# A hybrid diffusion layer on one core: where the last gate's modulation is summed, and which engine does five small groups of the mixer

## The chip, the core and the metric

The kernel runs on one core of one Trainium2 chip. The core has a matrix engine (TensorE, PE in the profile, with its weight loads as PEld), a vector engine (VectorE, DVE), a scalar engine (ScalarE, ACT), a general-purpose engine (GpSimd, POOL) and a synchronisation engine (SyncE, SP) that here only starts DMA transfers. Each engine works through its own instruction queue in order and waits on semaphores for the others. The metric is the device time of one execution in microseconds, the median of several runs.

## The reference, cut to what matters

One layer: a half-step SwiGLU FFN, a token mixer (grouped-query attention and a bidirectional mLSTM side by side), a second half-step SwiGLU FFN, a final RMSNorm. Every sub-layer is normalised and then shifted, scaled and gated by rows of a modulation vector, which has nine rows of 2048.

```python
D_MODEL = 2048; SEQ = 256; CTX_LEN = 256; HEAD_DIM = 128; N_MOD = 9

def adaln(x, g, mod, i):
    return rms_norm(x, g) * (1 + mod[:, i + 1, None, :]) + mod[:, i, None, :]

def half_step_ffn(x, mod, i, g, w_up, w_down):
    h = adaln(x, g, mod, i)
    a, b = jnp.split(h @ w_up, 2, axis=-1)
    return x + 0.5 * mod[:, i + 2, None, :] * ((jax.nn.silu(a) * b) @ w_down)

def reference(...):
    mod_l = (silu_c @ w_mod[l] + b_mod[l]).reshape(B, N_MOD, D_MODEL)
    xl = half_step_ffn(xl, mod_l, 0, ...)
    ...
    xl = xl + mod_l[:, 5, None, :] * mixer_output(att_l, hm_l, ...)
    xl = half_step_ffn(xl, mod_l, 6, ...)
    return rms_norm(xl, g_final)
```

Row 8 of the modulation is the gate of the second FFN: it is first used when the second FFN's last sums are gated. Row 5 gates the mixer's output, rows 6 and 7 shift and scale the second FFN's input. In the mLSTM, keys carry a factor of 128 to the power -0.5, ISQ in the kernel.

## The kernel before, in words

All weights are fp32. A product is made of three matmuls in the fp32r format: the weight is split into a rounded part `hi` and a rest `lo`, and hi times hi, hi times lo and lo times hi are summed (`mm3`, lines 145 to 149). The split of one weight tile of 128 x 2048 (`split`, lines 117 to 136) is made in two halves, each one ACTIVATE by ScalarE (line 125) and one subtraction by VectorE (line 126), into rings of four halves for hi and four for lo. `load_split` (line 138) loads a tile by SyncE, splits it, and lets a side stream called `beside["load"]` go one step.

The mixer (lines 1259 to 1855) projects in this order, each weight tile feeding 24 or 48 matmuls: w_c, w_a, w_b (values and gates of the mLSTM, four groups of tokens), w_mk and w_mq (keys and queries of the mLSTM, eight heads each, with a short convolution), w_kv, w_q0, w_o0, w_o1, w_q1 (attention and output gates), and the output projection w_out, three quarters of it first (`out_proj` with weights 2, 0, 3 for each of four column blocks), the last quarter after attention. Between the matmuls, generators are stepped by hand: mLSTM states, `latents`, `attention`, `evacs`. `tc.keep_in_program_order` ties an instruction behind the previous one traced on its engine; what is not tied may be moved by a list scheduler, which goes by its own estimate of when each instruction is ready.

The modulation rows 2 to 8 are not made by matmuls. For each row i, each block of 128 outputs (kt, 16 of them) and each half h of the 2048 inputs, a tile of 128 x 1024 of w_mod is loaded (512 KB) and VectorE multiplies it with the broadcast condition vector and sums along the row, in one SCALAR_TENSOR_TENSOR (`mod_half`, line 205). Such an instruction is called a pass here. Rows 2 to 4 are done in the first FFN (`mod_items`), rows 5 to 7 in the mixer (class `Beside`, lines 271 to 337), row 8 in the second FFN (`mod_late`, lines 264 to 269, stepped by `load_split` there). When all 32 passes of a row are done, `mod_end` adds halves and bias, and for a gate row `mod_rows_out` turns it by a transpose on TensorE and writes it to DRAM.

`Beside` holds its tiles in six buffers: sr0, sr1, sr2 and three that lie in memory which later stages need. Each buffer has a limit, the number of the first pass that may not use it: N_EARLY for the three that lie in mqT and rt, N_MIXER for sr1 and sr2. At the end of the mk stage `mods.close(N_EARLY)` issues all passes below that number, before the output projection `mods.close(N_MIXER)` does, and then three further buffers in mkT and C1 are added (line 1787). The pass order is h first, then row, then kt; at the change of h the condition vector is loaded again. A pass and the load into its buffer are tied to program order. When pass n is issued is set by PACE, pairs (n, step) that are interpolated; a step is taken after each contraction block of a projection with tokens still (16 steps each), after four of them in mk and mq (4 per head), and after each weight tile of the output projection (12). Each h adds WAIT = 3 steps.

```python
                    if self.n not in self.slots or self.done < np.interp(self.n, *zip((0, 0), *self.pace)) + self.waits:
                        break
                    self.one()
```

The second FFN (lines 1858 to 2253) interleaves blocks computed directly (`up`, `down`) with blocks by a seven-product scheme (`quad`), whose token forms (`token_forms`, line 2010) are made by VectorE and ScalarE at its start. `before_final` (line 2227) ends the side stream of row 8 and loads the gate row.

The five groups of the mixer that the change touches: `state` scales the values with the input gates into vw (line 1429) and copies the state C1 out of PSUM (line 1434); the mq stage multiplies the convolved query by ISQ (line 1552); `attention` scales the probabilities p by their inverse sum sd (line 1699); `mlstm_cat` copies transposed heads cx out of PSUM (line 1750). All are VectorE's. In `latents` VectorE multiplies A with the query (line 1509) and E with the scores pS (line 1514).

Of the kernel before, what the change touches and what calls it, by code (L numbers as in the profile page):

```python
# [9 lines left out]
F32 = mybir.dt.float32  # L10
# [3 lines left out]
AF = mybir.ActivationFunctionType  # L14
ALU = mybir.AluOpType
# [4 lines left out]
P = 128  # L20
D = 2048
KT = D // P
T = 256
# [12 lines left out]
PACE = (4, 2), (12, 13), (19, 19), (26, 28), (33, 37), (37, 44), (42, 51), (48, 54), (52, 61), (55, 70), (58, 76), (59, 85), (63, 96)  # L36
PACE += (70, 102), (72, 109), (75, 118), (76, 130), (77, 144), (80, 152), (83, 163), (85, 166), (86, 174), (96, 181)

# [18 lines left out]
def tile_layer(ctx: ExitStack, tc: tile.TileContext, I: dict, out: bass.AP):  # L57
# [205 lines left out]

    def mod_late(sp, i0, i1, pace):

        cB = sp.tile([P, 1024], F32, name="cBl", bufs=1)
        cond = Conditions(lambda h: h, lambda h: conditions({LAT: cB}, h, h + 1, (LAT,)), lambda h: {LAT: cB})
        raws = lambda: sp.tile([P, 1024], F32, tag="sraw", name="sraw", bufs=2)
        return mod_items(half_items(i0, i1), nc.sync.dma_start, raws, 2, cond, None, pace)
# [131 lines left out]
    def drain(it):  # L401
        for _ in it:
            pass
# [855 lines left out]
    with ExitStack() as mx:  # L1259
# [31 lines left out]
        N_EARLY, N_MIXER = 50, 85  # L1291

        early2 = one([P, 2, 1024], "early2", tag="mqT")
        tiles = [(mm.tile([P, 1024], F32, name="sr0"), 96)] + [(mm2.tile([P, 1024], F32, name=f"sr{j}"), N_MIXER) for j in (1, 2)]
        tiles += [(x, N_EARLY) for x in (early2[:, 0, :], early2[:, 1, :], one([P, 1024], "early1", tag="rt"))]
        mods = Beside(mm, 5, 8, tiles, PACE)
# [122 lines left out]
        def state(h, kTc):  # L1419
# [7 lines left out]
            for t in range(2):  # L1427
                for d in range(2):
                    nc.vector.tensor_scalar(vw[:, t, d, :], v1[CTX][t][:, h, :], wg[:, t, d, h : h + 1], None, op0=ALU.mult)
# [4 lines left out]
            nc.vector.tensor_copy(C1[:, h, :, :], b[:, :260].rearrange("p (d c) -> p d c", d=2))  # L1434
# [39 lines left out]
        def latents():  # L1474
            held = {}
            for h in range(NH + 1):
                if h < NH:
# [31 lines left out]
                    nc.vector.tensor_tensor(A, A, mqT[:, h, :].unsqueeze(1).to_broadcast([P, 2, T]), op=ALU.mult)  # L1509
                    for d in range(2):  # L1510

                        for w, p0 in ((slice(0, 2), 0), (slice(2, 3), 3)) if d == 0 else ((slice(0, 1), 0), (slice(1, 3), 2)):
                            e_ = E[:, d, w, :]
                            nc.vector.tensor_tensor(e_, e_, pS.rearrange("p (q c) -> p q c", q=4)[:, p0 : p0 + w.stop - w.start, :], op=ALU.mult)
# [26 lines left out]
        for h in range(NH):  # L1541
# [8 lines left out]
            nc.scalar.activation(y, y, AF.Silu)  # L1550

            nc.vector.tensor_scalar(mqT[:, h, :], y, ISQ, None, op0=ALU.mult)
# [130 lines left out]
        def attention(kv):  # L1683
            items = [(t, g) for t in range(2) for g in range(4)]
            pr, pT, o = {}, {}, {}
            for i in range(len(items) + 2):
                if i < len(items):
# [11 lines left out]
                    nc.vector.tensor_scalar(p, p, sd, None, op0=ALU.mult)  # L1699
# [42 lines left out]
        def mlstm_cat(c):  # L1742

            for t in range(2):
# [5 lines left out]
                nc.vector.tensor_copy(cxs[c, t], tb)  # L1750
# [657 lines left out]
```

## Time and profile before

| | |
|---|---|
| median of three runs | 2613.49 us (2612.78 to 2615.28) |
| span of the profiled execution, first to last instruction | 2612.7 us |
| granted TensorE clock, mean over the span | 0.996 |
| HBM read, written | 659.87 MB, 17.89 MB |
| mean DMA rate over the span | 259 GB/s |
| mixer, projection a to the end of the output projection | 1395.7 to 1895.8 us |
| passes on VectorE in that stretch | 96, of 1.22 us each |

The profiled execution's time is shown by its span alone; the timed runs are 0.04 to 2.5 us above it. Times in the profile are counted from the first instruction of the span. A row of a group reads: line of the kernel, engine, operation, output<-inputs with their shapes, count; then busy us, mean ns of one, and the idle time of the engine just before such instructions with what ended it. A row of the timeline reads: start, duration (both us), engine, line, operation, names and shapes; in square brackets the engine's idle time before it and what ended it. Matmuls overlap their successors, so their durations exceed the distance between their starts.

### The profile page before, as it was taken

Reading aid. Unit: us, or ns where it says so; the run is one execution under the profiler, and the core shown is the slowest. Engines: PE = TensorE matmul, PEld = TensorE weight load, DVE = VectorE, ACT = ScalarE, POOL = GpSimd, SP = SyncE. Lnnn points to the kernel's source line nnn. Section 1 sums busy time; section 2 is a strip of 40 time slices with the busy share of each in tenths; the row PEclk is TensorE's granted clock in tenths of the full one; section 3 lists DMA queues with packets and bytes.
Section 4 is the critical chain, followed back from the end, with each engine's and each line's share of the span. In section 5 each row is a group of like instructions: output and inputs, shape, how many; then the busy total and the mean of one; then the engine's idle time right before and its main releaser. Section 6 shows DMA issues by size and latency. Waiting matters only on the chain.

```text
span 2612.7 us, 33775 instructions
## 1 busy us (share of the span) xinstructions
PE 2590.1 (99%) x12742; PEld 2158.4 (83%) x12742; DVE 2119.7 (81%) x2860; ACT 1364.8 (52%) x1734; POOL 205.2 (8%) x261
## 2 busy tenths in 40 slices
PE   8999999999999999999999999999999999999998
PEld 5788888888888888888889889888898888888887
DVE  7788888878888788888887879788888777777867
ACT  4454444454444465444454337555576655555554
POOL 0000000100000100010110000120000000000001
PEclk8999999999999999999999999999999999999999
DMA  9989999999999998889987856665679998989975
GB/s 389 353 215 266 280 273 274 257 273 284 265 277 277 271 246 237 231 200 232 231 247 262 300 193 236 220 214 208 236 254 302 309 293 278 286 285 283 270 231 174
DMA packets 127219, 679.97 MB, mean 260 GB/s; under 512 B 14152, under 2 KB 16712, under 8 KB 65232
## 3 DMA queue, kind: packets, MB, share of 16 engines
q1 hardware_dynamic: 99696, 500.59, 51.6%
q0 software_dynamic: 27360, 177.22, 34.7%
q8 instruction: 100, 1.64, 0.2%
q14 instruction: 63, 0.52, 0.1%
HBM read 659.87 MB, written 17.89 MB: 259 GB/s over the span
## 4 chain that ended last, share of the span: by engine, by line
PE 92%; DVE 3%; DMA 2%; issue 1%; ACT 1%; POOL 0%; ACTq 0%; POOLq 0%; SPq 0%; DVEq 0%
PE mm L147 24%; PE mm L149 24%; PE mm L148 24%; PE mm L85 2%; PE tr L147 2%; PE tr L149 2%; PE tr L148 2%; PE Y L149 1%; PE Y L147 1%; PE Y L148 1%; PE tr L85 1%; PE X L147 1%; PE X L149 1%; PE X L148 1%; DVE lo L126 1%
## 5 line engine op out<-in xcount | busy, mean ns | idle before, releaser
L125 ACT ACTIVATE hi<-raw 128x1024 fp32r<-128x1024 f32 (+3 forms) x536 | 556.4, 1042 | 594.7 <-PE mm L149 435.4
L126 DVE TENSOR_TENSOR lo<-raw,hi 128x1024 fp32r<-128x1024 f32 (+1 forms) x524 | 632.1, 1211 | 272.3 <-ACT hi L125 246.9
L125 ACT ACTIVATE hi<-chain 128x1024 fp32r<-128x1024 f32 x320 | 338.0, 1059 | 257.3 <-PE mm L149 133.9
L126 DVE TENSOR_TENSOR lo<-chain,hi 128x1024 fp32r<-128x1024 f32 x320 | 386.5, 1221 | 85.4 <-ACT hi L125 82.3
L147 PE MATMUL mm<-hi,hhi 128*128 128x512 f32 (+3 forms) x1024 | 393.8, 385 | 0.0
L148 PE MATMUL mm<-lo,hhi 128*128 128x512 f32 (+3 forms) x1024 | 386.8, 378 | 0.0
L149 PE MATMUL mm<-hi,hlo 128*128 128x512 f32 (+3 forms) x1024 | 386.8, 378 | 0.0
L205 DVE SCALAR_TENSOR_TENSOR junk<-sraw,cBh 128x1024 fp8e5<-128x1024 f32 x192 | 234.4, 1221 | 16.8 <-DMA sraw<-in_w_mt 14.4
L149 PEld LDWEIGHTS mm<-hi,hlo 128*128 128x128 f32 x1024 | 192.5, 188 | 33.9
L147 PEld LDWEIGHTS mm<-hi,hhi 128*128 128x128 f32 x1024 | 192.6, 188 | 31.0
L148 PEld LDWEIGHTS mm<-lo,hhi 128*128 128x128 f32 x1024 | 192.8, 188 | 30.6
L149 PE MATMUL mm<-hi,hid2l 128*128 128x512 f32 x352 | 137.4, 390 | 0.0
L147 PE MATMUL mm<-hi,hid2h 128*128 128x512 f32 x352 | 137.2, 390 | 0.0
L148 PE MATMUL mm<-lo,hid2h 128*128 128x512 f32 x352 | 137.1, 389 | 0.0
L148 PE MATMUL mm<-lo,h2hi 128*128 128x512 f32 x320 | 124.9, 390 | 0.6 <-DVE lo L126 0.6
L147 PE MATMUL mm<-hi,h2hi 128*128 128x512 f32 x320 | 124.8, 390 | 0.0
L149 PE MATMUL mm<-hi,h2lo 128*128 128x512 f32 x320 | 124.6, 389 | 0.0
L735 POOL DMA_DIRECT2D chain<-in_w_up1b x60 | 53.1, 886 | 726.4 <-DVE lo L126 699.5
L147 PE MATMUL mm<-hhi,hi 128*128 128x512 f32 (+1 forms) x288 | 101.1, 351 | 0.0
L149 PE MATMUL mm<-hhi,lo 128*128 128x512 f32 (+1 forms) x288 | 99.0, 344 | 0.0
L148 PE MATMUL mm<-hlo,hi 128*128 128x512 f32 (+1 forms) x288 | 98.8, 343 | 0.0
L205 DVE SCALAR_TENSOR_TENSOR sr<-sr,cBl 128x1024 f32<-128x1024 f32 x65 | 78.4, 1219 | 9.0 <-DMA sr<-in_w_mt 9.0
(517 smaller groups left out, 5466.9 us busy)
## 6 DMA issues: line engine op xcount, KB each, us to landing
raw<-in_w_dn SPq DMA_DIRECT2D x70, 1024.0 KB, 7.7
sraw<-in_w_mt SPq DMA_DIRECT2D x128, 512.0 KB, 7.7
chain<-in_w_up1b POOLq DMA_DIRECT2D x60, 1024.0 KB, 10.4
raw<-in_w_up2b SPq DMA_DIRECT2D x50, 1024.0 KB, 6.9
raw<-in_w_up1b SPq DMA_DIRECT2D x40, 1024.0 KB, 7.7
mraw<-in_w_m SPq DMA_DIRECT2D x32, 1024.0 KB, 7.8
sr<-in_w_mt SPq DMA_DIRECT2D x62, 512.0 KB, 5.4
chain<-in_w_dn POOLq DMA_DIRECT2D x30, 1024.0 KB, 9.4
```

The source lines that it names most:

```text
L85: ins = getattr(self.engine, name)(*a, **k)
L125: scalar[0].activation(hi, src, AF.Copy)
L126: vector[0].tensor_tensor(lo, src, hi.bitcast(F32), op=ALU.subtract)
L147: tensor[0].matmul(out_ap, sh, mh, start=first, stop=False, skip_group_check=skip)
L148: tensor[0].matmul(out_ap, sh, ml, start=False, stop=False, skip_group_check=skip)
L149: tensor[0].matmul(out_ap, sl, mh, start=False, stop=last, skip_group_check=skip)
L205: ins = nc.vector.scalar_tensor_tensor(junk() if junk else raw, raw, 1.0, cB[s], op0=ALU.mult, op1=ALU.mult, accum_out=mT[:, i, s, kt, h : ...
L735: accum = lambda dst, src: nc.gpsimd.dma_start(dst, src, accum_op=ALU.add)
```

## The change

Row 8 joins rows 5 to 7 in the mixer: `Beside(mm, 5, 9, ...)` has 128 passes in place of 96, in halves of 64. PACE is a new list, N_EARLY goes from 50 to 62, N_MIXER from 85 to 109, the last limit from 96 to 128. `mod_late`, its pool and its draining in `before_final` are gone; `load_split` still steps an empty `beside["load"]`. The scalings of vw and p and the copies of C1 and cx become ACTIVATE Copy instructions of ScalarE. The multiplication of the query by ISQ is gone: Silu writes mqT directly, and the factor is folded into the multiplications of lines 1509 and 1514, which become SCALAR_TENSOR_TENSOR.

```diff
@@ -33,8 +33,8 @@
 
 N_IDLE = 4
 
-PACE = (4, 2), (12, 13), (19, 19), (26, 28), (33, 37), (37, 44), (42, 51), (48, 54), (52, 61), (55, 70), (58, 76), (59, 85), (63, 96)
-PACE += (70, 102), (72, 109), (75, 118), (76, 130), (77, 144), (80, 152), (83, 163), (85, 166), (86, 174), (96, 181)
+PACE = (4, 2), (12, 13), (19, 19), (27, 28), (35, 37), (41, 44), (49, 51), (56, 54), (62, 61), (67, 70), (70, 76), (71, 85), (76, 96)
+PACE += (83, 102), (87, 109), (91, 118), (94, 130), (97, 144), (101, 152), (107, 163), (110, 170), (128, 181)
 
 PACE2 = 70 / 73
 
@@ -260,13 +260,6 @@
     left = {i: 2 * KT for i in range(2, 9)}
 
     half_items = lambda i0, i1: [(i, kt, h) for h in range(2) for i in range(i0, i1) for kt in range(KT)]
-
-    def mod_late(sp, i0, i1, pace):
-
-        cB = sp.tile([P, 1024], F32, name="cBl", bufs=1)
-        cond = Conditions(lambda h: h, lambda h: conditions({LAT: cB}, h, h + 1, (LAT,)), lambda h: {LAT: cB})
-        raws = lambda: sp.tile([P, 1024], F32, tag="sraw", name="sraw", bufs=2)
-        return mod_items(half_items(i0, i1), nc.sync.dma_start, raws, 2, cond, None, pace)
 
     class Beside:
 
@@ -1288,12 +1281,12 @@
         mm = mmcm.__enter__()
         mm2cm = pool(name="mm2", bufs=1)
         mm2 = mm2cm.__enter__()
-        N_EARLY, N_MIXER = 50, 85
+        N_EARLY, N_MIXER = 62, 109
 
         early2 = one([P, 2, 1024], "early2", tag="mqT")
-        tiles = [(mm.tile([P, 1024], F32, name="sr0"), 96)] + [(mm2.tile([P, 1024], F32, name=f"sr{j}"), N_MIXER) for j in (1, 2)]
+        tiles = [(mm.tile([P, 1024], F32, name="sr0"), 128)] + [(mm2.tile([P, 1024], F32, name=f"sr{j}"), N_MIXER) for j in (1, 2)]
         tiles += [(x, N_EARLY) for x in (early2[:, 0, :], early2[:, 1, :], one([P, 1024], "early1", tag="rt"))]
-        mods = Beside(mm, 5, 8, tiles, PACE)
+        mods = Beside(mm, 5, 9, tiles, PACE)
         beside["part"] = mods.steps()
         ev_mv(6, 0, b_c)
         b_a = {}
@@ -1426,12 +1419,12 @@
             vw = m1.tile([P, 2, 2, 130], F32, tag="E", name="vw")
             for t in range(2):
                 for d in range(2):
-                    nc.vector.tensor_scalar(vw[:, t, d, :], v1[CTX][t][:, h, :], wg[:, t, d, h : h + 1], None, op0=ALU.mult)
+                    nc.scalar.activation(vw[:, t, d, :], v1[CTX][t][:, h, :], AF.Copy, scale=wg[:, t, d, h : h + 1])
             yield
             b = bank()
             for t in range(2):
                 nc.tensor.matmul(b[:, :260], kn[:, t, :], vw[:, t, :, :], start=t == 0, stop=t == 1)
-            nc.vector.tensor_copy(C1[:, h, :, :], b[:, :260].rearrange("p (d c) -> p d c", d=2))
+            nc.scalar.activation(C1[:, h, :, :], b[:, :260].rearrange("p (d c) -> p d c", d=2), AF.Copy)
             yield
 
         def channels(name, h, N, b):
@@ -1506,12 +1499,12 @@
                             channel_multiplier=1 if d else -1,
                         )
                     yield
-                    nc.vector.tensor_tensor(A, A, mqT[:, h, :].unsqueeze(1).to_broadcast([P, 2, T]), op=ALU.mult)
+                    nc.vector.scalar_tensor_tensor(A, A, ISQ, mqT[:, h, :].unsqueeze(1).to_broadcast([P, 2, T]), op0=ALU.mult, op1=ALU.mult)
                     for d in range(2):
 
                         for w, p0 in ((slice(0, 2), 0), (slice(2, 3), 3)) if d == 0 else ((slice(0, 1), 0), (slice(1, 3), 2)):
                             e_ = E[:, d, w, :]
-                            nc.vector.tensor_tensor(e_, e_, pS.rearrange("p (q c) -> p q c", q=4)[:, p0 : p0 + w.stop - w.start, :], op=ALU.mult)
+                            nc.vector.scalar_tensor_tensor(e_, pS.rearrange("p (q c) -> p q c", q=4)[:, p0 : p0 + w.stop - w.start, :], ISQ, e_, op0=ALU.mult, op1=ALU.mult)
                     held[h] = E, A
                     yield
                 if h:
@@ -1547,9 +1540,7 @@
                 if n % 2 and (h, n) not in ((1, 1), (1, 3)):
                     steps(lat)
             y = conv(b, h, 1)
-            nc.scalar.activation(y, y, AF.Silu)
-
-            nc.vector.tensor_scalar(mqT[:, h, :], y, ISQ, None, op0=ALU.mult)
+            nc.scalar.activation(mqT[:, h, :], y, AF.Silu)
             ready[0] = h + 1
 
 
@@ -1696,7 +1687,7 @@
                     sd = sm.tile([P, 1], F32, tag="sd", name="sd")
                     nc.scalar.activation(p, b, AF.Exp, scale=ISQ, bias=nm, accum_out=sd)
                     nc.vector.reciprocal(sd, sd)
-                    nc.vector.tensor_scalar(p, p, sd, None, op0=ALU.mult)
+                    nc.scalar.activation(p, p, AF.Copy, scale=sd)
                     pr[i] = p
                 if 0 <= i - 1 < len(items):
                     p = pr.pop(i - 1)
@@ -1747,7 +1738,7 @@
                     o = (4 * c + g) * P
                     nc.tensor.transpose(tb[:, g * P : (g + 1) * P], hm[:, t, o : o + P], ident)
                 cxs[c, t] = m1.tile([P, 512], F32, tag="nM", name="cx")
-                nc.vector.tensor_copy(cxs[c, t], tb)
+                nc.scalar.activation(cxs[c, t], tb, AF.Copy)
                 yield
 
         bo = ({}, {})
@@ -1784,7 +1775,7 @@
         mods.close(N_MIXER)
         mm2cm.__exit__(None, None, None)
         late2 = one([P, 2, 1024], "late2", tag="mkT")
-        mods.more([(late2[:, 0, :], 96), (late2[:, 1, :], 96), (one([P, 1024], "late1", tag="C1"), 96)], nc.sync)
+        mods.more([(late2[:, 0, :], 128), (late2[:, 1, :], 128), (one([P, 1024], "late1", tag="C1"), 128)], nc.sync)
         hcm.__exit__(None, None, None)
 
 
@@ -1985,8 +1976,6 @@
         f3 = ctx.enter_context(pool(name="f3", bufs=1, side="right"))
         acc2 = f2.tile([P, 2, D], F32, name="acc2", bufs=1)
         chain_ = [f3.tile([P, 2048], F32, tag=f"c{q}", name=f"chain2{q}") for q in range(2)]
-        f8cm = pool(name="f8", bufs=1)
-        beside["load"] = mod_late(f8cm.__enter__(), 8, 9, ((32, 62),))
 
 
         LAST = NF // FB - 1
@@ -2225,8 +2214,6 @@
             yield from down(8)
 
         def before_final():
-            drain(beside["load"])
-            f8cm.__exit__(None, None, None)
             late["g8"] = f3.tile([P, D], F32, tag="c0", name="g8")
             late["gf"] = f3.tile([P, D], F32, tag="c1", name="gf")
             nc.sync.dma_start(late["g8"], mod_rows[8][LAT, :].partition_broadcast(P))
```

## The prediction

> **What bounds the kernel now.** I read the page's first part, then its chain of waits, then a table of stages.
>
> ```profile
> PE 2590.1 (99%) x12742; PEld 2158.4 (83%) x12742; DVE 2119.7 (81%) x2860; ACT 1364.8 (52%) x1734; POOL 205.2 (8%) x261
> PE 92%; DVE 3%; DMA 2%; issue 1%; ACT 1%; POOL 0%; ACTq 0%; POOLq 0%; SPq 0%; DVEq 0%
> ```
>
> TensorE is busy in 2590.1 of 2612.7 us and 92% of the chain that ended last is its work. The change leaves every matmul in place, so only TensorE's idle time can be won. The stage table shows where that is. Its columns are the stretch, its length, busy us of PE, PEld, DVE, ACT and POOL with counts, then the granted clock, DMA share and GB/s. The rows are: projections a and b; mk; mq; kv; q0 with o0; o1 with q1; the first three quarters of the output projection (out3 below); (its last quarter left out); the start of the second FFN; the second FFN in two parts; the sum, the left-out row included.
>
> ```profile
> core 0: us, PE busy (x) PEld busy (x) DVE busy (x) ACT busy (x) POOL busy (x), PEclk, DMA share, GB/s
> 1395.70:1468.50 72.80, 72.80 (x414) 71.69 (x413) 56.89 (x115) 22.73 (x33) 1.35 (x3) 1.00 0.90 328
> 1468.50:1564.20 95.70, 95.68 (x429) 78.20 (x427) 72.82 (x129) 36.85 (x58) 0.00 (x0) 1.00 0.68 237
> 1564.20:1619.60 55.40, 55.40 (x449) 54.67 (x448) 51.68 (x105) 44.90 (x80) 2.74 (x8) 1.00 0.65 226
> 1619.60:1669.70 50.10, 50.10 (x244) 42.03 (x242) 35.04 (x84) 22.99 (x46) 2.88 (x7) 1.00 0.68 239
> 1669.70:1726.20 56.50, 56.50 (x297) 47.97 (x296) 48.37 (x106) 35.24 (x65) 15.76 (x23) 1.00 0.58 201
> 1726.20:1787.20 61.00, 61.00 (x322) 51.63 (x320) 48.88 (x80) 35.12 (x51) 6.08 (x5) 1.00 0.66 229
> 1787.20:1871.70 84.50, 84.48 (x426) 70.30 (x425) 70.17 (x114) 42.59 (x60) 3.31 (x4) 1.00 0.63 218
> ...
> 1895.80:1977.00 81.20, 80.76 (x543) 74.78 (x542) 73.73 (x109) 58.33 (x88) 3.31 (x6) 1.00 0.80 269
> 1977.00:2400.00 423.00, 422.39 (x1885) 348.70 (x1884) 320.44 (x336) 240.40 (x252) 26.16 (x30) 1.00 0.94 290
> 2400.00:2604.00 204.00, 203.40 (x913) 167.88 (x911) 161.68 (x186) 107.95 (x120) 14.51 (x17) 1.00 0.77 234
> sum 1208.30, PE 1206.60 PEld 1027.74 DVE 961.59 ACT 665.38 POOL 76.10; mean PE 109.69 PEld 93.43 DVE 87.42 ACT 60.49 POOL 6.92
> ```
>
> From the mixer to the end of the second FFN TensorE idles 1208.3 - 1206.6 = 1.7 us. A busy engine could still be slow, so I also looked at the distance between matmul starts.
>
> ```profile
> 2300.36 0.39 PE L149 MATMUL mm<-hi,hid2l 128*128 128x512 f32 x1
> 2300.58 0.39 PE L147 MATMUL mm<-hi,hid2h 128*128 128x512 f32 x1
> ...
> 1868.53 0.39 PE L148 MATMUL mm<-lo,cathi 128*128 128x512 f32 x1
> 1868.76 0.39 PE L149 MATMUL mm<-hi,catlo 128*128 128x512 f32 x1
> ```
>
> The start-to-start distance is 0.22 to 0.23 us in the second FFN (DMA share 0.94) and 0.23 in the mixer (0.63): it does not follow the load of the other engines. So a gain above about 2 us has no place in this profile, while a loss has: VectorE is 70 to 93% busy in the mixer's stages and the change gives it more.
>
> **The change part by part.** VectorE's groups that matter in the mixer, then, from the view of one tile, the passes of the second FFN (ns lowest, median, highest; first and last start):
>
> ```profile
> L205 DVE SCALAR_TENSOR_TENSOR sr<-sr,cBl 128x1024 f32<-128x1024 f32 x65 | 78.4, 1219 | 9.0 <-DMA sr<-in_w_mt 9.0
> L1699 DVE TENSOR_SCALAR pr<-pr,sd 128x512 f32<-128x512 f32 x16 | 7.7, 485 | 0.4
> L1429 DVE TENSOR_SCALAR vw<-v1c,wg 128x130 f32<-128x130 f32 x32 | 7.6, 281 | 0.0
> L1434 DVE COPY C<-mm 128x260 f32<-128x260 f32 x8 | 3.4, 422 | 0.0
> L1750 DVE COPY cx<-tr 128x512 f32<-128x512 f32 x4 | 2.7, 685 | 1.1 <-PE tr L1748 1.1
> L1552 DVE TENSOR_SCALAR mqT<-cy 128x256 f32<-128x256 f32 x8 | 2.3, 291 | 0.4 <-ACT cy L1550 0.2
> ```
>
> ```profile
> L205 DVE SCALAR_TENSOR_TENSOR sraw<-sraw,cBl x32: 1217/1218/1222, 1970.6 to 2494.8; 128x1024 f32<-128x1024 f32 x32
> ```
>
> *Passes.* 32 passes of 1.22 us, 39.0 us of VectorE, leave the second FFN for the mixer, with 32 loads of 512 KB on SyncE's queue. Out of VectorE's mixer work go 7.7 + 7.6 + 3.4 + 2.7 + 2.3 = 23.7 us. Net: +15.3 us in the mixer. The ISQ factor folded into L1509 and L1514 turns a two-operand pass into a three-operand one over the same elements; on equal tiles both forms take the same (lo splits and passes, 1.21 to 1.23 each in the timeline rows below), so 0; 40 such instructions at those 0.02 us of difference are 0.8 us either way.
>
> Where the passes land comes from PACE: the pair (n, step) says that pass n is due at that step, steps between are interpolated, and each of the two halves of w_mod waits 3 steps more. Steps: a and b 32, mk 32, mq 32, kv 16, q0 and o0 32, o1 and q1 32, out3 12. Walking both lists, passes issued by the end of these seven are 27, 50, 61, 71, 77, 86, 96 before, and 28, 62, 73, 85, 96, 110, 128 after. By stage that adds 1, 11, 0, 2, 5, 5, 8. VectorE's load then is its row plus 1.22 each less what moved away there: In a and b 56.9 + 1.2 = 58.1 of 72.8 (80%). In mk, where seven of the eight states run and so 7/8 of 11.0 = 9.6 goes, 72.8 + 13.4 - 9.6 = 76.6 of 95.7 (80%). In mq 51.7 - 1.4 - 2.3 = 48.0 of 55.4 (87%). In kv 35.0 + 2.4 = 37.4 of 50.1 (75%). In q0 and o0 48.4 + 6.1 = 54.5 of 56.5 (96%). In o1 and q1, where half the softmax scalings and copies go (5.2), 48.9 + 6.1 - 5.2 = 49.8 of 61.0 (82%). In out3 70.2 + 9.8 - 5.2 = 74.8 of 84.5 (88%).
>
> No stage passes 100%, so what counts is how early each weight half is split before TensorE wants it. The two tightest places:
>
> ```profile
> 1686.56 1.21 DVE L126 TENSOR_TENSOR lo<-raw,hi 128x1024 fp32r<-128x1024 f32 x1
> ...
> 1691.40 0.39 PE L147 MATMUL mm<-hi,hhi 128*128 128x512 f32 x1
> ...
> 1803.19 1.22 DVE L126 TENSOR_TENSOR lo<-raw,hi 128x1024 fp32r<-128x1024 f32 x1
> ...
> 1805.15 0.39 PE L147 MATMUL mm<-hi,cathi 128*128 128x512 f32 x1
> ```
>
> And the passes alone in the first 30 us of out3 (VectorE's busy us and count):
>
> ```profile
> 1787.20:1817.20 30.00, 0.00 (x0) 1.00 0.53 188
> ```
>
> In q0 a split ends at 1687.77 and is used at 1691.40: 3.6 us spare. The five added passes are 6.1 us over q0 and o0, of which VectorE's own idle there (56.5 - 48.4 = 8.1) can take all. Bounds: 0 if it does, 6.1 - 3.6 = 2.5 if it takes none; I take 0, because the added work is spread over 32 steps. In out3 the third weight tile's second half ends at 1804.41 and is used at 1805.15: 0.7 us spare. Before, no pass ran there until 1817; now passes 110 and 111 are due after the first and second tiles, so 2.4 us come ahead of this split and the two copies of cx (1.4) go: 2.4 - 1.4 - 0.7 = **+0.3**. Bounds: 0, and 2.8 with passes 112 and 113 ahead of it too (4 x 1.22 - 1.4 - 0.7).
>
> *ScalarE.* It gets 32 scalings of 130 columns, 8 copies of 260, and 16 and 4 of 512. Nearest rows:
>
> ```profile
> L1494 ACT ACTIVATE E<-nM,u 128x128 f32<-128x128 f32 x32 | 12.3, 391 | 2.3 <-PE mm L1433 1.2 <-issue 1.0
> L1425 ACT ACTIVATE kn<-tr 128x256 f32<-128x256 f32 x8 | 3.1, 384 | 4.2 <-PE tr L1423 4.2
> L1806 ACT ACTIVATE cathi<-cx 128x512 fp32r<-128x512 f32 x4 | 2.4, 624 | 0.3 <-DVE cx L1750 0.2
> ```
>
> 32 x 0.391 + 8 x 0.384 + 20 x 0.624 = 28.1 us. Its fullest stage, mq (44.9 of 55.4), gets one state's part, 4 x 0.391 + 0.384 = 1.9: 46.8, or 85%. The new wait is that ScalarE, after each softmax Exp, waits for VectorE's reciprocal before it scales; queued behind it are hi splits, then the lo splits that need them. ScalarE waits for VectorE there already (nm, then Exp), and the reciprocal follows at once: 0, or 16 x 0.624 = 10.0 if nothing covers it. Cover is the spare above plus ScalarE's idle half.
>
> *Second FFN.* It loses 39.0 us of VectorE and 16.8 MB. What that is worth is read from its one stall:
>
> ```profile
> 1970.62 1.22 DVE L205 SCALAR_TENSOR_TENSOR sraw<-sraw,cBl 128x1024 f32<-128x1024 f32 x1
> ...
> 1971.76 1.23 DVE L2012 TENSOR_TENSOR ra<-h2hi 128x1024 f32<-128x1024 f32 x1
> ...
> 1977.44 1.22 DVE L126 TENSOR_TENSOR lo<-raw,hi 128x1024 fp32r<-128x1024 f32 x1
> ...
> 1977.71 0.40 PE L147 MATMUL mm<-hi,h2hi 128*128 128x512 f32 x1
> 1978.72 0.50 PE L148 MATMUL mm<-lo,h2hi 128*128 128x512 f32 x1 [0.61 <-DVE lo L126]
> ```
>
> Those two matmuls start 1.01 apart instead of 0.23: 0.78 lost to a lo split that stands behind one pass in a full VectorE queue. Without the pass it ends 1.14 earlier (the next instruction's start, 1971.76, less 1970.62): **-0.8**. Bounds: 0 and -1.7, all the idle time above. The transposes that write the gate's row move into the mixer: their number stays, 0.
>
> Sum: 2612.7 + 0.3 - 0.8 = 2612.2 by the profiled span. The median of the runs stands 0.8 above that span (2613.49), so **2613.0**.
>
> One rule of the Trainium skill speaks against a floor at 0.227. "TensorE: Matmul & The Clock Gate", section "Wait — 56ns, not 53.3ns?", gives 215.7 ns start to start for 512 columns at full clock. The trace shows 0.22 to 0.23 us at a granted clock of 1.00 throughout, so here the measurement decides.
>
> **The rivals.** *VectorE becomes the bound from q0 to out3* (slower). For: 167.4 of these 202.0 us are busy, each idle stretch waits for another engine, and passes hold a fixed place in the order. Against: TensorE never waited in them. It decides once the work ahead of a split exceeds that split's spare, 0.7 to 3.6 us at the tight places. Added are 6.1 + 0.9 + 4.6 = 11.6 us; if half the gaps can't take them, 5.8 reach TensorE: **2619**; if none can, less 0.7, **2624**.
>
> *The refills come late.* In out3 the passes have four buffers and some 1.6 passes per weight tile (24 matmuls, 5.4 us); I count seven refills issued one tile ahead of their pass.
>
> ```profile
> late<-in_w_mt SPq DMA_DIRECT2D x7, 512.0 KB, 6.7
> ```
>
> At 6.7 to landing each such pass holds VectorE 1.3 us, 8.8 in all; the 5.4 us of a tile ahead cover most: +3.4, **2616.4**. For: the share of the DMA there is only 0.63, against.
>
> *The second FFN's matmuls run closer together* once passes and loads are gone (faster): its 1885 + 913 matmuls, if each lost 0.01 us to the others' load, give 28 us: **2585**. Against: the equal distances above, at different loads. With the skill's 215.7 an estimate comes to about 31 us.
>
> *The change does not do what it says*: the stall at 1977 stays, since the token forms fill VectorE by themselves: 2613.8.
>
> **How the numbers follow.** The forecast has 0.60, with its own range 2611 to 2615.5 (the 1.7 us bound below; 2.5 above). VectorE as the bound 0.25, late refills 0.08, faster matmuls 0.03, the stall that stays 0.04. I call 0.2% (5.2 us) what a measurement of this kernel can tell from no change. Slower: 0.25 and a third of the refills, 0.28. Faster: 0.03 and 0.02 out of the forecast for what the trace hides, 0.05. Within: 0.67. The range goes from 2610.5 to 2619.5: it leaves out the far half of the VectorE case and the faster matmuls.
>
> **What would show it.** Right: PE idle between 1395 and 2604 stays under 3 us; VectorE near 96% in q0 and o0; no gap between the matmuls at the start of the second FFN. Wrong: gaps of TensorE in q0, o0 or out3 that end on lo (VectorE's bound), on lo after a pass that waited for its load (refills), or on a transpose of pr (ScalarE's wait); matmul distances in the second FFN under 0.22.

## The result, and the profile after

The changed kernel takes 2618.74 us (median of seven runs, 2616.4 to 2625.7) against 2613.1 (seven runs, 2612.49 to 2615.28): a ratio of 1.0026, with the 95% interval 1.0015 to 1.0036. It is slower, by a little more than the 0.2% that the prediction called the limit of what can be told. Measured a second time beside the experiments, unaltered, it had 1.0021 [1.0012, 1.003].

From the page of the changed kernel: the engines' busy time, the chain that ended last, and the group of passes.

```profile
PE 2593.1 (99%) x12742; PEld 2159.5 (83%) x12742; DVE 2099.3 (80%) x2792; ACT 1393.4 (53%) x1798; POOL 208.8 (8%) x261
...
PE 92%; DVE 3%; DMA 3%; issue 1%; ACT 1%; POOL 0%; SPq 0%; ACTq 0%; POOLq 0%; DVEq 0%
...
L205 DVE SCALAR_TENSOR_TENSOR sr<-sr,cBl 128x1024 f32<-128x1024 f32 x85 | 102.8, 1219 | 14.7 <-DMA sr<-in_w_mt 14.4
```

The bound is where it was: TensorE, 92% of the chain. The span is 2616.0 us, 3.3 longer. To see where it grew I took the start of TensorE's n-th instruction in both traces, for both have 12742 of them in nearly the same order, and watched the difference. At the first matmul of the mixer the changed kernel is 1.8 us ahead, which lies before anything that was changed: the profiled execution of the kernel before had a spell of 3.4 us at half clock at 39.9 us, the other had none there. From there to the last one it loses 5.0 us: 0.7 in mk, 5.2 in o1 and q1, and it wins 0.7 in the second FFN; no other stage moves by more than 0.2. The same stages in the table of windows of the changed kernel (mk; q0 with o0; o1 with q1; out3; the second FFN's first part), their ends set at the matmuls of the same numbers:

```profile
1466.70:1563.40 96.70, 95.95 (x430) 78.49 (x429) 78.67 (x115) 48.45 (x91) 0.00 (x0) 1.00 0.85 303
...
1668.60:1724.90 56.30, 56.30 (x296) 47.79 (x295) 53.56 (x119) 35.19 (x64) 12.75 (x17) 1.00 0.73 250
1724.90:1791.40 66.50, 63.35 (x322) 53.01 (x321) 49.09 (x79) 43.47 (x63) 11.02 (x11) 0.97 0.71 250
1791.40:1875.70 84.30, 84.30 (x426) 69.63 (x425) 74.49 (x122) 48.32 (x70) 3.13 (x3) 1.00 0.77 270
...
1980.80:2403.20 422.40, 422.34 (x1886) 348.93 (x1885) 293.87 (x285) 240.49 (x252) 26.10 (x30) 1.00 0.88 258
```

q0 with o0, where VectorE is fullest (53.56 of 56.30, 95%), has no idle TensorE at all. o1 with q1, where VectorE is only 74% busy, took 61.30 us before and takes 66.50: TensorE is idle for 66.50 - 63.35 = 3.15 of it, and the granted clock is 0.97. What TensorE waited for between 1340 and 2010, in the view of waits of the changed kernel (in total, times, longest):

```profile
PE tr L1696 <- ACT pr L1690: 3.2, 2, 2.3
PE mm L1426 <- ACT kn L1418: 0.6, 1, 0.6
PE mm L442 <- ACT hi L125: 0.4, 1, 0.4
```

and of the kernel before:

```profile
PE mm L148 <- DVE lo L126: 0.6, 1, 0.6
PE mm L449 <- ACT hi L125: 0.4, 1, 0.4
```

The wait on lo, the stall at the start of the second FFN, is gone. New are two waits on pr, the softmax probabilities, and one on kn, the transposed keys of the mLSTM. Attention works in items: one block of 128 x 512 scores goes through maximum, Exp, reciprocal and scaling, and then through four transposes on TensorE. The longer wait on pr, in the second item, in the timeline of the changed kernel:

```profile
1741.64 0.68 DVE L1684 TENSOR_REDUCE nm<-mm 128x1 f32<-128x512 f32 x1
...
1742.24 1.21 DVE L205 SCALAR_TENSOR_TENSOR sr<-sr,cBl 128x1024 f32<-128x1024 f32 x1
...
1743.62 0.69 ACT L1688 ACTIVATE pr<-mm,nm 128x512 f32<-128x512 f32 x1 [0.92 <-DVE nm L1685]
...
1744.24 1.23 DVE L205 SCALAR_TENSOR_TENSOR sr<-sr,cBl 128x1024 f32<-128x1024 f32 x1 [0.71 <-DMA sr<-in_w_mt]
...
1745.39 1.22 DVE L126 TENSOR_TENSOR lo<-raw,hi 128x1024 fp32r<-128x1024 f32 x1
1746.52 0.15 DVE L1689 RECIPROCAL sd<-sd 128x1 f32<-128x1 f32 x1
...
1746.71 0.72 ACT L1690 ACTIVATE pr<-pr,sd 128x512 f32<-128x512 f32 x1 [2.31 <-DVE sd L1689]
...
1747.49 0.66 PE L1696 MATMUL tr<-ident,pr 128*128 128x128 f32 x4 [2.26 <-ACT pr L1690]
```

and the end of the same item in the kernel before:

```profile
1742.87 0.67 ACT L1697 ACTIVATE pr<-mm,nm 128x512 f32<-128x512 f32 x1
1742.99 1.23 DVE L126 TENSOR_TENSOR lo<-raw,hi 128x1024 fp32r<-128x1024 f32 x1 [0.83 <-ACT hi L125]
...
1744.13 0.15 DVE L1698 RECIPROCAL sd<-sd 128x1 f32<-128x1 f32 x1
...
1744.33 0.49 DVE L1699 TENSOR_SCALAR pr<-pr,sd 128x512 f32<-128x512 f32 x1
...
1745.07 0.60 PE L1705 MATMUL tr<-ident,pr 128*128 128x128 f32 x4
```

Read the reciprocal in both. Exp ends near 1743.5 before, and the reciprocal follows 0.6 later behind one lo split; the scaling ends at 1744.82 and the transposes start at 1745.07, so there were 0.26 us to spare. After, Exp starts 0.75 us later by the time of the span: one pass stands between the maximum and its scaling in both kernels, but the maximum itself comes later. Then a second pass stands behind Exp, for whose load VectorE waits 0.71, then the lo split: the reciprocal comes 2.2 us behind Exp's end at 1744.31, and TensorE stands for 2.26.

The idle time is 3.15 of the 5.2 us. Most of the rest is in a window of the changed kernel just behind that wait; 0.50, the number behind the five engines, is the granted clock:

```profile
1749.00:1752.00 3.00, 3.00 (x8) 2.32 (x8) 0.87 (x3) 1.50 (x3) 0.00 (x0) 0.50 0.82 270
```

For 3.41 us, by the trace's clock records, TensorE works at half its clock, which costs another 1.7; some 0.4 us of the stage stay unexplained. So one late block of probabilities cost 2.26 + 1.7 = 4.0 us.

### The profile page after: what moved, and what is told of

Its sections match the earlier page's. It is cut to its first block, busy times and chain, and to the rows that moved or that the text cites. A ratio compares the mean times of both kernels' runs of the same rounds, so it can differ in the third digit from the quotient of the medians.

```text
span 2616.0 us, 33774 instructions
## 1 busy us (share of the span) xinstructions
PE 2593.1 (99%) x12742; PEld 2159.5 (83%) x12742; DVE 2099.3 (80%) x2792; ACT 1393.4 (53%) x1798; POOL 208.8 (8%) x261
## 4 chain that ended last, share of the span: by engine, by line
PE 92%; DVE 3%; DMA 3%; issue 1%; ACT 1%; POOL 0%; SPq 0%; ACTq 0%; POOLq 0%; DVEq 0%
PE mm L147 24%; PE mm L149 24%; PE mm L148 24%; PE mm L85 2%; PE tr L148 2%; PE tr L149 2%; PE tr L147 2%; PE Y L149 1%; PE Y L148 1%; PE Y L147 1%; DMA mraw<-in_w_m 1%; PE X L147 1%; PE X L149 1%; PE X L148 1%; PE tr L85 1%; DVE lo L126 1%
## 5 line engine op out<-in xcount | busy, mean ns | idle before, releaser
L205 DVE SCALAR_TENSOR_TENSOR sr<-sr,cBl 128x1024 f32<-128x1024 f32 x85 | 102.8, 1219 | 14.7 <-DMA sr<-in_w_mt 14.4
```

The source lines that it names most:

```text
L205: ins = nc.vector.scalar_tensor_tensor(junk() if junk else raw, raw, 1.0, cB[s], op0=ALU.mult, op1=ALU.mult, accum_out=mT[:, i, s, kt, h : ...
```

## The experiments

Three theories run through the expectations. By the first (A) a pass that PACE puts ahead of a maximum or a reciprocal in attention makes pr late. By the second (B) it is ScalarE's queue: the scaling of p, or kn, stands behind a hi split. By the third (C) VectorE's work in the mixer is too much in sum. All results in one table. The ratio is to the kernel before in the same runs (its medians were 2613.1 for the first row, 2614.5 for e1 to e4, 2612.82 for c0, e6, e7 and e9, 2613.3 for e8 and e11 to e13). The columns behind it are us lost in the profiled execution against the profiled execution of before, by the n-th instruction of TensorE as above: from the mixer's start to the end, and of that in mk, in o1 with q1, and in the second FFN from 1977 to 2400.

| kernel | median us | ratio [95%] | all | mk | o1, q1 | FFN |
|---|---|---|---|---|---|---|
| changed kernel | 2618.74 | 1.0026 [1.0015, 1.0036] | 5.0 | 0.7 | 5.2 | -0.7 |
| e1 | 2617.89 | 1.0016 [1.0007, 1.0025] | 7.3 | 0.7 | 4.9 | -0.6 |
| e2 | 2616.15 | 1.0007 [0.9998, 1.0016] | 1.5 | 0.6 | 1.2 | -0.8 |
| e3 | 2616.55 | 1.0010 [1.0001, 1.0018] | 2.4 | 0.8 | 1.8 | -0.2 |
| e4 | 2621.2 | 1.0026 [1.0015, 1.0037] | 6.2 | 1.3 | 5.2 | -0.8 |
| c0, changed kernel again | 2618.21 | 1.0021 [1.0012, 1.003] | 4.8 | 2.7 | 3.4 | -0.9 |
| e6 | 2614.88 | 1.0008 [0.9999, 1.0017] | 1.5 | 2.6 | 0.4 | -1.0 |
| e7 | 2614.84 | 1.0007 [0.9998, 1.0016] | 1.6 | 0.8 | 0.2 | 0.0 |
| e9 | 2612.52 | 1.0001 [0.9992, 1.001] | 0.9 | 0.0 | 0.1 | 0.0 |
| e8 | 2616.26 | 1.0009 [1.0, 1.0018] | 4.6 | 0.1 | 4.1 | -0.1 |
| e11 | 2612.93 | 0.9995 [0.9986, 1.0004] | -0.6 | 0.0 | 0.0 | -0.8 |
| e12 | 2616.55 | 1.0013 [1.0004, 1.0022] | 1.6 | 0.0 | 1.8 | -0.2 |
| e13 | 2613.32 | 1.0 [0.9991, 1.0008] | 0.0 | 0.0 | 0.0 | 0.0 |

By the times alone only the changed kernel (both rows), e1, e3, e4 and e12 are clear of the kernel before; e8 touches it, and e2, e6, e7, e9, e11 and e13 can't be told from it. The columns of losses are finer, but show one execution each: those of e3 (2614.63 us) and e4 (2618.73) were the fastest of their kernels. Outside the last three columns, e7, e8 and e9 lose 0.5 to 0.8 us near 1906 on a wait for a hi split, in a stage that their edits don't touch.

**The two halves of the change (e3, e4).** e3 is the kernel before with the five groups and the ISQ factor as in the changed kernel, row 8 left in the second FFN.

> The kernel before with only the five groups moved (vw, C1, p and cx on ScalarE, ISQ folded into the two multiplications); row 8 stays in the second FFN with the old PACE. Theory A: as before within 1 us (2612.5 to 2614), no wait on pr over 0.3 us. Theory B: waits on pr of 1 us or more, 2615 or more.

e4 is the changed kernel with row 8 in the mixer and the new PACE, but with those groups as before.

> The changed kernel with all five groups given back to VectorE: only row 8 is moved, with the new PACE. Theory A: waits on pr as in the changed kernel, and more waits on lo or pr where VectorE has 24 us more work; 2617 to 2625. Theory B: no wait on pr over 0.5 us; 2612 to 2614 if VectorE's load alone does no harm.

e4 alone is as slow as the whole change. TensorE's waits on pr in e4, where VectorE scales p:

```profile
PE tr L1698 <- DVE pr L1692: 5.1, 5, 2.0
```

e3 costs less, 2.4 us, and has no gain in the second FFN to set against it (-0.2), since row 8 stays there. It has the wait on pr that theory B expected of it. Its waits:

```profile
PE tr L1703 <- ACT pr L1697: 1.5, 1, 1.5
PE mm L1433 <- ACT kn L1425: 1.0, 1, 1.0
```

So the moved passes carry most of the loss, and the groups have a smaller one of their own.

**The scaling of p (e1, e8).** e1 gives that scaling back to VectorE in the changed kernel, e8 gives it alone to ScalarE in the kernel before:

```diff
# e1, against the changed kernel; e8, against the kernel before, is the reverse
-                    nc.scalar.activation(p, p, AF.Copy, scale=sd)
+                    nc.vector.tensor_scalar(p, p, sd, None, op0=ALU.mult)
```

> The changed kernel with one group given back: the softmax probabilities are scaled by VectorE again, all else as changed. Theory A (passes stand between the row maximum and the reciprocal in VectorE's order, so p is late whoever scales it): TensorE still waits about 1 and 2 us for the transposes of pr in o1, some microseconds of half clock follow the longer wait, and the time stays 3 to 6 us above before (2616 to 2620). Theory B (the new wait of ScalarE for the reciprocal, and its slower scaling, make p late): the waits on pr fall under 0.5 us together and the time is within 1.5 us of before.

> The kernel before with the scaling of p alone on ScalarE. Theory B in its part on the attention: a hi split stands between Exp and the scaling, TensorE waits once on pr near 1763, 1.0 to 1.5 us, none on kn near 1488 since vw and C1 are VectorE's; time 1 to 2 us above the kernel before. If the reciprocal follows at once and something covers the scaling, as the prediction took it: no wait over 0.5 and the time of before.

In e1 TensorE waits on pr for 4.2 us in four places in place of 3.2 in two: the stalls do not come from ScalarE's scaling. (Its total of 7.3 has another 2.2 between the end of q1 and 1977 that the edit does not explain: two waits for a hi split near 1910, 1.5 us together, and a spell of 3.4 us at half clock behind them.) In e8 theory B's stall comes at its place, in the fifth item, longer than expected. Timeline of e8:

```profile
1763.16 0.69 ACT L1697 ACTIVATE pr<-mm,nm 128x512 f32<-128x512 f32 x1 [3.19 <-DVE nm L1694]
...
1763.84 1.04 ACT L125 ACTIVATE hi<-raw 128x1024 fp32r<-128x1024 f32 x1
1763.97 0.16 DVE L1698 RECIPROCAL sd<-sd 128x1 f32<-128x1 f32 x1 [0.18 <-ACT pr L1697]
1764.79 0.71 ACT L1699 ACTIVATE pr<-pr,sd 128x512 f32<-128x512 f32 x1
...
1765.55 0.66 PE L1705 MATMUL tr<-ident,pr 128*128 128x128 f32 x4 [2.24 <-ACT pr L1699]
```

Here the reciprocal is on time (1763.97), and ScalarE has taken a hi split of 1.04 us first. Two different engines make the same kind of stall at different items. The half clock follows again, in a window of e8:

```profile
1766.00:1769.00 3.00, 3.00 (x14) 2.54 (x13) 2.16 (x6) 2.30 (x6) 0.00 (x0) 0.62 0.63 186
```

2.24 idle and 1.7 from the clock make 3.9 of the 4.1 us lost.

**The groups of the state alone (e7).** The kernel before with only the scaling into vw and the copy of C1 on ScalarE, lines 1429 and 1434.

> The kernel before with vw and C1 alone on ScalarE. Theory A: one wait of TensorE for kn of about 1 us near 1488, none on pr over 0.3 us, so about 1 us above before. Theory C: no wait, since ScalarE is busy only 39% of that stage.

The wait on kn, the keys copied out of PSUM for the state, is there by itself (1.0 us, none on pr), and 0.8 us are lost in mk. Where it comes from is seen in the timeline of the changed kernel:

```profile
1488.50 1.05 ACT L125 ACTIVATE hi<-raw 128x1024 fp32r<-128x1024 f32 x1
...
1489.45 0.37 ACT L1418 ACTIVATE kn<-tr 128x256 f32<-128x256 f32 x1
...
1489.87 0.70 PE L1426 MATMUL mm<-vw,kn 128*128 128x260 f32 x2 [0.56 <-ACT kn L1418]
```

kn stands behind a hi split; before, kn started at 1488.50 with nothing ahead of it, and the matmul came at 1490.60 without a wait. Leaving these groups on VectorE does not save mk once the passes are there: e4 loses 1.3 us in it, with a wait of 0.8 on another kn near 1526.

**Fewer passes in o1 (e2, e6).** e2 is the changed kernel with passes due earlier, so that 97 in place of 94 are due by step 130:

```diff
-PACE += (83, 102), (87, 109), (91, 118), (94, 130), (97, 144), (101, 152), (107, 163), (110, 170), (128, 181)
+PACE += (83, 102), (87, 109), (91, 116), (97, 130), (100, 139), (101, 154), (107, 163), (110, 170), (128, 181)
```

> The changed kernel with another PACE: passes 95 to 100 are due in kv, q0 and o0 and none is due from step 146 to 157, so that none stands before the first three reciprocals of the softmax in VectorE's order; the five groups stay with ScalarE. Theory A: no wait on pr in o1, clock 1.00 there, time 2612 to 2614. Theory B: the waits on pr stay at 2 us or more and the time at 2616 or more. If VectorE's load in q0 and o0 is the bound (it was reckoned at 96% without these passes), waits on lo appear there.

e6 is e2 with vw, C1 and p back on VectorE.

> The version with the earlier passes, with vw, C1 and p given back to VectorE; cx stays with ScalarE and ISQ stays folded. Theory A (two losses: passes ahead of the reciprocals, and ScalarE's in-order queue ahead of kn and p): no wait over 0.5 us on kn or pr, no stall at the start of the second FFN, so before minus 0.8, within 1 us of before in any case. Theory C (VectorE's total load in the mixer sets the loss, wherever the passes stand): with 18 us more on VectorE than the earlier version, waits on pr or lo appear again and the time is 2 us or more above before.

In e2 both stalls at the start of o1 are gone, and 1.2 us are lost there where 5.2 were; one wait on pr of 1.0 us is left near 1767, and the time, 2616.15, misses the 2612 to 2614 of theory A. The passes brought forward cost something where they went: e2 loses 0.9 us in q0 with o0, on no lo split but on another chain of small steps, the denominators den of the mLSTM. Timeline of e2:

```profile
1702.44 1.22 DVE L205 SCALAR_TENSOR_TENSOR sr<-sr,cBl 128x1024 f32<-128x1024 f32 x1
...
1703.58 0.15 DVE L1527 TENSOR_TENSOR den<-tr,den 128x2 f32<-128x2 f32 x1
...
1704.93 0.35 PE L1522 MATMUL tr<-v1l,E 128*128 128x130 f32 x1 [0.64 <-DVE den L1527]
```

In e6 the wait near 1767 goes too (0.2). e6 also answers theory C for o1. VectorE's busy time from 1468.5 to 1895, the third of the busy columns in a window, in the changed kernel:

```profile
1468.50:1895.00 426.50, 422.59 (x2240) 359.88 (x2240) 359.62 (x638) 256.19 (x433) 34.77 (x44) 1.00 0.75 262
```

and in e6:

```profile
1468.50:1895.00 426.50, 423.89 (x2253) 361.56 (x2252) 378.28 (x700) 237.24 (x390) 38.64 (x44) 1.00 0.75 264
```

e6 has 18.7 us more VectorE work in the same stretch than the changed kernel, and loses 0.4 us in o1 in place of 5.2. What it still loses is 2.6 us in mk, and there VectorE is late: TensorE waits 1.65 us for cy, the convolved keys, and 0.8 for a kn near 1527. Timeline of e6:

```profile
1482.99 1.22 DVE L205 SCALAR_TENSOR_TENSOR early<-early,cBl 128x1024 f32<-128x1024 f32 x1
...
1484.13 2.32 DVE L1409 SCALAR_TENSOR_TENSOR cy<-mm,vecs,cy 128x510 f32<-128x510 f32 x3
...
1486.52 1.28 ACT L1457 ACT_TABLE_LOAD   x1 [7.11 <-DVE cy L1409]
```

VectorE had been busy without a gap since 1470.5, with seven passes and the scalings into vw of two states ahead of or between the steps of cy, and ScalarE stood 7.11 us for them before its Silu. So theory C is out for o1, but in mk e6 leaves open whether the sum of VectorE's work or the place of the passes makes cy late. The time, 2.1 us above the kernel before, misses theory A's 1 us and lies where theory C put it, for a stall in another stage.

**A delay put in by hand, a miss (e9).** The kernel before with four idle reductions pinned between nm and the reciprocal of the second item:

```diff
-                    nc.vector.reciprocal(sd, sd)
+                    if kv == 0 and i == 1:
+                        for _ in range(4):
+                            pin(nc.vector.tensor_reduce(sm.tile([P, 1], F32, tag="nm", name="nm"), b, axis=AX.X, op=ALU.max))
+                    pin(nc.vector.reciprocal(sd, sd))
```

> The kernel before, with four idle row maxima of 0.68 us each put between the Exp and the reciprocal of the second softmax item, 2.7 us of VectorE at one place and no pass moved. Theory A: TensorE waits 1.5 to 2.7 us for that item's pr and the time rises by that much, or 1.7 us more where the clock halves. Theory C: 2.7 us in 600 is hidden by VectorE's idle time; no wait, no change.

No wait on pr came, and 2612.52 us is the time of the kernel before. The list scheduler knew of the reductions and put TensorE's transposes of that item later, from 1745.07 to 1748.01, with other matmuls ahead of them, so that 0.37 us were still spare. Here a delay that the scheduler reckoned with was scheduled around. e9 therefore says nothing against theory A, but it was the wrong instrument.

**The passes themselves, put in and taken out (e12, e13).** So I moved passes in the kernel before, by one line of PACE and with nothing else touched. e12 brings three passes into the start of o1, which gives its second item the order of VectorE that the changed kernel has, and its first item a pass at the same two places; e13 takes three out.

```diff
 before  (72, 109), (75, 118), (76, 130), (77, 144), (80, 152), (83, 163), (85, 166)
 e12     (72, 109), (75, 118), (76, 130), (79, 144), (83, 152), (84, 163), (85, 166)
 e13     (75, 109), (78, 118), (79, 130), (79.5, 144), (80, 152), (83, 163), (85, 166)
```

> The kernel before with one line of PACE changed: three passes that were due behind step 144 are due between 130 and 152, so that VectorE has one pass ahead of the first reciprocal of the o1 stage and two between the maximum and the reciprocal of the second item, as in the changed kernel. No row is moved, no group is moved, and the passes are as many as before. Theory A (passes ahead of the softmax chain make pr late): TensorE waits on pr near 1740 and 1748, 2 to 5 us in all, the time is 2615 to 2618, the wait of 0.6 at 1977 stays, and no wait on kn near 1488. Theory B (ScalarE's queue) and theory C (VectorE's sum of work in the mixer): neither is changed, so no wait on pr over 0.5 and a time within 1 us of the kernel before.

> The control of the one before: the kernel before with the same line of PACE changed the other way, three passes out of the o1 stage's first half into kv and q0, so that no pass stands in the first item and one in the second. Theory A: no wait on pr, as before, and the time of the kernel before within 1.5 us; the spare of the second item's probabilities rises from 0.26 us only if a pass leaves that item. If moving passes by itself, wherever to, costs time (late loads, or lo splits in kv and q0): waits of TensorE on lo there, and 2615 or more.

Timeline of e12, the second item:

```profile
1743.59 0.19 ACT L1697 ACTIVATION_READ_ACCUMULATOR pr<-mm,nm 128x1 f32 x1
...
1743.85 1.23 DVE L205 SCALAR_TENSOR_TENSOR sr<-sr,cBl 128x1024 f32<-128x1024 f32 x1 [0.96 <-DMA sr<-in_w_mt]
...
1745.00 1.22 DVE L126 TENSOR_TENSOR lo<-raw,hi 128x1024 fp32r<-128x1024 f32 x1
...
1746.14 0.16 DVE L1698 RECIPROCAL sd<-sd 128x1 f32<-128x1 f32 x1
...
1746.96 0.63 PE L1705 MATMUL tr<-ident,pr 128*128 128x128 f32 x4 [1.57 <-DVE pr L1699]
```

It is the stall of the changed kernel again, the late load included, in a kernel with no row moved, no group moved and as many passes as before. It loses 1.8 us in o1 by the profile and 3.2 us by the medians (2616.55 less 2613.3). The first item did not stall, so the sum of waits, 1.6 us, lies under the 2 to 5 that were expected. A pass and three lo splits stand ahead of that item's maximum in both kernels; but in the changed kernel VectorE had stood 2.85 us for GpSimd's gm, a factor of the mLSTM's output, before them, in e12 2.06. What makes the changed kernel's 0.89 us there was not tried. Nor was a pass in the same place with its load in time: in the second item VectorE waits 0.96 us for that load in e12 and 0.71 in the changed kernel, so by estimate 0.6 of the 1.57 and 1.55 of the 2.26 us would be left without it. e13, with as many passes moved the other way, has the median of before to 0.02 us: moving passes costs nothing by itself. Theory A, late loads included, holds for the larger part; in o1 the place decides, not the number.

**The gain alone (e11).** The kernel before, with row 8 left in the second FFN but begun eight weight tiles later:

```diff
-        beside["load"] = mod_late(f8cm.__enter__(), 8, 9, ((32, 62),))
+        beside["load"] = itertools.chain([None] * 8, mod_late(f8cm.__enter__(), 8, 9, ((32, 54),)))
```

> The kernel before with row 8's passes in the second FFN begun eight weight tiles later and ended at the same one; nothing in the mixer is touched. This is the one gain of the change by itself: no wait on lo near 1977 and 0.6 to 0.8 us less than the kernel before (2612.0 where that is 2612.8), which is less than an interval can tell. If the token forms fill VectorE by themselves the wait stays and the time is that of before.

The wait on lo is gone and 0.8 us are won between 1977 and 2400 in the trace, as much as the change wins there, with the mixer untouched. 2612.93 us gives the lowest ratio of all, 0.9995, but its interval reaches from 0.9986 to 1.0004, so it can't be told from the kernel before. It is clearly faster than the changed kernel.

**The changed kernel again (c0).**

> The changed kernel once more, unaltered, beside the versions of this call. Theory A and B alike: 3 to 6 us above before; the trace shows the waits on pr at 1738 and 1745 again, and a spell of half clock in some executions only, so its times scatter by several microseconds.

The waits on pr are there again (3.0 us, the longest 2.15 in the trace), but this time the clock stayed at 1.00 behind them, and a wait that the first execution nearly did not have (0.2 us) came to 2.2 in mk. Timeline of c0:

```profile
1489.06 1.06 ACT L125 ACTIVATE hi<-raw 128x1024 fp32r<-128x1024 f32 x1 [8.20 <-DMA raw<-in_w_mk]
...
1492.21 0.44 PE L1416 MATMUL tr<-ident,cy 128*128 128x128 f32 x2 [2.23 <-ACT cy L1458]
```

A tile of w_mk landed late, ScalarE stood 8.20 us for it, and the Silu that makes cy was queued behind. e6 waits for the same instruction (1.65 us), but by the way shown above, through VectorE; the kernel before has no such wait. The DMA share in mk is 0.85 in the changed kernel against 0.68 in the prediction's row for about the same stretch, so added loads are a likely cause of the late tile, but no kernel tried mk's loads by themselves. That part stays open, and with it some of the scatter between executions.

## Why the prediction was wrong, step by step

**The bound and the ceiling.** Right. No kernel here gained more than 1.0 us in the second FFN, and the matmul distances there did not change: the same 1886 instructions took 422.40 us after and 423.20 before, and the difference is that of the stall.

**The second FFN, -0.8.** Right in place, cause and size: -0.7 in the changed kernel, -0.8 in e11 alone; e12 and e13, which leave it, keep the wait of 0.6. The rival by which the stall stays is out.

**Where the passes land and how full VectorE gets.** Nearly right: 81% in mk, 95% in q0 with o0, 88% in out3, for 80, 96 and 88 forecast; mq came to 93%, for 87, without a wait of TensorE. In o1 with q1 the 49.8 us of work forecast were 49.09. The factor ISQ folded into two groups cost nothing, as forecast: 5.5 and 9.4 us after, 5.6 and 9.5 before.

**The lo splits, +0.3 in out3.** A term that did not matter: no kernel with the moved passes waited longer than 0.2 us on a lo split between 1340 and 2010, and from the end of q1 to the end of the mixer the changed kernel loses nothing (-0.1).

**The step that failed** is the sentence "No stage passes 100%, so what counts is how early each weight half is split before TensorE wants it". It took the lo splits for the only work of VectorE with a deadline, looked at their spare (3.6 and 0.7 us), and so priced the five passes added in o1 and q1 at nothing. A tighter deadline was that of the probabilities, 0.26 us in the second item of attention, and that chain passes VectorE three times (maximum, its scaling, reciprocal; a fourth where VectorE scales p), each time behind what is already queued. In place of 0 the stage lost 5.2 us: 3.15 of waits on pr, 1.7 from the clock, the rest unexplained. Of the 3.15 the 2.26 of the second item are shown to come from passes and their late load (e12); the 0.89 of the first went away when passes were moved (e2, e6), but came with the wait on gm too.

**ScalarE, "the reciprocal follows at once: 0, or 10.0 if nothing covers it".** The value 0 was wrong and the bound held. In the changed kernel the reciprocal did not follow at once, since a pass and a lo split stood ahead of it; and where it did, in e8, a hi split stood ahead of the scaling and the loss was 4.1 us. In the whole change this stall does not show: its two waits on pr are in the first two items, and e1, without ScalarE's scaling, still has them. That it hides behind them is likely and was not tried. The move of vw and C1, priced with the rest as covered, costs 0.8 in mk (e7), where the changed kernel loses 0.7 at the same instruction.

**The sum.** 0.7 in mk, 5.2 in o1 with q1, -0.7 in the second FFN, and -0.2 in all else, are the 5.0 us of the profile; the medians differ by 2618.74 - 2613.1 = 5.6. The prediction put 0.8 us between a span and its run's time; in every run of the result they lie 1.7 apart (2617.73 and 2616.0 us), so the profiled execution of the kernel before was itself slower than its median. The forecast does not hang on this: it is the median before, less 0.5.

**The rivals.** "VectorE becomes the bound", at 2619, came out with nearly the right time by luck: from q0 to out3 its mechanism did not act, for there was no wait on lo, and e6 with more VectorE work lost less there. That the time lies inside the stated range of 2610.5 to 2619.5 is the same luck, since the range reached that far for this rival's sake. "The refills come late" saw a real thing in the wrong stage; its 8.8 us already took a tile's 5.4 off each of the seven refills, and taking 5.4 off once more, to 3.4, counted it twice. The view of the tile sr, 1500 to 1900, says in its line of idle time how often passes waited for their loads, after:

```profile
  DMA sr<-in_w_mt: 7.8, 6
```

against 1.8 us in one pass before. These waits held VectorE, and one of them, 0.71 us, stood in the chain at 1744; in out3 they cost TensorE nothing. The sign to watch for, gaps on a transpose of pr, was named, but put down to ScalarE's wait alone.

## What to carry to other kernels

When work is added to an engine that has idle time, list every chain of small steps that crosses that engine and ends at the bounding one, with its spare, and not only the bulk stream; here a stage at 74% stalled and one at 95% did not, until three more passes in it met the steps of den (e2). A softmax step of 0.15 us is as late as the 1.2-us instruction ahead of it, so filler work belongs where no such chain is open (e13). And before moving work to win a stall, try to shift it by a few steps where it is: e11 had the whole gain, 0.8 us by the trace, for nothing.

## What the hardware showed that was not expected

An idle time of 2.26 us (changed kernel) and of 2.24 us (e8) was followed by 3.41 us at half the granted clock; 1.96 us (e4) and 2.15 us (c0) at the same stage were not, with the clock at 1.00. So a stall of some 2.2 us can cost 1.7 us more. Its length alone does not decide: the wait of 2.23 us in mk of c0, shown above, was not followed by half clock, and in e1 waits of 1.01 and 0.44 us near 1910 were. In each trace the clock's changes lie on one grid of 3.41 us, and the idle time within one interval of that grid sorts the cases of the mixer: 2.26 (changed kernel) and 2.21 (e8) were followed, while c0's 2.15 and 2.23 are cut by the grid into 1.74 and 0.41 and into 1.08 and 1.15, e4's 1.96 into 1.34 and 0.62, and e1's 1.81 in its second item was not enough. The 1.45 near 1910 in e1 does not fit, so this is a reading of the traces and not a rule.

The Trainium skill, "TensorE: Matmul & The Clock Gate", section "Part 1: The HAM clock gate (the "warmup" mystery)", gives 3413 ns as the window of the clock gate and half clock as its idle state, and the traces agree with both numbers. It lets the clock fall after at least one idle window of about 3.4 us; here 2.24 us was enough, so for the idle time the measurement decides. The page says that the window runs freely, which makes the outcome depend on when a stall begins; the grid and the cut stalls of c0 fit that.
